# Hybrid encoder layer on one core: the output projection as seven half-size products, with its weight sums kept in DRAM

## The chip, the cores and the metric

The kernel runs on one core of a Trainium2 chip. The metric is the device time of one execution in microseconds (us), as the median of several runs. TensorE (PE in the profile) multiplies; VectorE (DVE), ScalarE (ACT) and GpSimd (POOL) do the element-wise work; SyncE (SP) issues most of the transfers.

## The reference

One layer of an encoder over 1024 tokens of 1024 features, all in float32:

```
u   = x @ W_in
mix = concat(retention(u), windowed_attention(u))     # 8 + 8 heads of 64
h   = LN1(alpha * x + mix @ W_out)
f   = SwiGLU(h) + sigmoid(h @ W_pg) * (p @ W_pe)
out = LN2(alpha * h + f)
```

The change concerns `mix @ W_out`, the product of two 1024x1024 matrices, and LN1 behind it. What follows directly, `h @ W_pg` (the gate) and `p @ W_pe` (the embedding, whose 256 inputs a token are few), plays a part in the order of work.

## The kernel before, in words

A float32 product is made of three passes of a split operand: each operand is a rounded high part and the low rest (`split`, L74: a ScalarE copy writes the high part, L75, a VectorE subtraction the low part, L76), and `mm3` (L81 to L83) multiplies high by high, high by low and low by high into one bank of PSUM. A matmul takes 128 rows of the inner index and makes 128 tokens by 512 features. There are eight banks, two each of the tags mm, s, t and o.

The mixers (retention and attention, four pairs) run first. TensorE's order there is laid down by hand: large matmuls are queued and `take` pulls some of them between the small ones; `side` holds small jobs that are given out at a count of such ticks. One kind of side job prepares weights: `put` splits a sum of weight slices on ScalarE and VectorE and SyncE writes both parts to DRAM. The gate's weights are prepared so (`presplit_gate`), because the gate is calculated by seven products of half-size matrices in place of eight, on sums of quarters of h and of W_pg.

The output projection has 8 inner slices (KT), 8 token tiles and 2 halves of the features. The mixers' output is split on the spot and so are the 8 slices of W_out, after they are loaded. The first four token tiles go together, slice by slice, into all eight banks; then tiles 4 to 7 one after another into two banks. `zpart` (L753) adds a tile to alpha times x, `ln_stats` takes its statistics, and `ln1_apply` does LN1: a power on GpSimd (L763) and two VectorE passes (L768, L769). `to_hT` transposes a tile on TensorE (L784, into banks) and splits it (L785, L786) into the four quarters HB of h. LN1 and transposes of tiles 0 to 3 lie in the middle of the products of tiles 4 to 7; tiles 4 and 5 are transposed behind the projection, tiles 6 and 7 inside gate product 1.

Then the gate. `product` (L891 to L893) multiplies four token tiles by four slices of one operand, into four banks; gate product 1 and product 2 share a set of banks (mm, s), product 5 has the other (t, o). Between the tiles of product 2 stand the embedding tiles (`first_tile`, `embed`): six matmuls into a bank of t or o, a sigmoid on ScalarE, a multiplication by the bank on VectorE (L948), an addition (L950). `t_sums` makes the operand sums of the gate's further products on VectorE (L860 to L867), each split in turn; product 5 needs the first of them, TT[1], which takes in all eight tiles of h. The SwiGLU part follows and takes more than half of the kernel's time.

Up to gate product 1 only TensorE's order in the mixers is by hand; from there on TensorE's and SyncE's order is as written. The other engines' orders are made by a scheduler: each engine works strictly in its own order.

## Time and profile before

| | |
|---|---|
| median of 3 runs | 1204.29 us (1204.23 to 1205.2) |
| the profiled execution | 1208.0 us, span 1206.2 us |
| granted TensorE clock, mean | 0.998 |
| TensorE busy | 1192.5 us |
| output projection on TensorE | 375.36 to 466.61 us |
| first matmul of gate product 1, of product 5 | 468.27, 497.39 us |
| hardware-issued DMA, GpSimd-issued DMA | 160.61 MB, 16.78 MB |

The profile is of one execution; its times count from the span's start. Rows of the timeline have the start, the length, the engine, the line, the operation, output and inputs by their names (buffer numbers left out), the shape, and in brackets the idle time ahead and what ended it. A matmul's length includes the drain of its pipeline, so that matmuls overlap; the distance between starts is what one takes.

### The profile page before, as it was taken

Reading aid. Unit: us, or ns where it says so; the run is one execution under the profiler, and the core shown is the slowest. Engines: PE = TensorE matmul, PEld = TensorE weight load, DVE = VectorE, ACT = ScalarE, POOL = GpSimd, SP = SyncE. Lnnn points to the kernel's source line nnn. Section 1 sums busy time; section 2 is a strip of 40 time slices with the busy share of each in tenths; the row PEclk is TensorE's granted clock in tenths of the full one; section 3 lists DMA queues with packets and bytes.
Section 4 is the critical chain, followed back from the end, with each engine's and each line's share of the span. In section 5 each row is a group of like instructions: output and inputs, shape, how many; then the busy total and the mean of one; then the engine's idle time right before and its main releaser. Section 6 shows DMA issues by size and latency. Waiting matters only on the chain.

```text
span 1206.2 us, 16452 instructions
## 1 busy us (share of the span) xinstructions
PE 1192.5 (99%) x5940; PEld 994.1 (82%) x5940; DVE 735.6 (61%) x1262; ACT 507.6 (42%) x958; POOL 363.1 (30%) x342
## 2 busy tenths in 40 slices
PE   9999999999999999999999999999999999999997
PEld 6888888888888888888888888888888888888885
DVE  4633788866645387946855554455554565775677
ACT  4665237665775124303423323233323324562463
POOL 2001020202010021001765565646656432034232
PEclk9999999999999999999999999999999999999999
DMA  6233635410103216656233222332133159999976
GB/s 249 83 110 141 249 135 195 151 40 20 35 18 122 91 50 229 255 202 220 89 132 131 79 79 105 131 132 79 63 121 131 70 178 300 375 274 218 258 178 199
DMA packets 70034, 178.45 MB, mean 148 GB/s; under 512 B 8128, under 2 KB 12352, under 8 KB 69952
## 3 DMA queue, kind: packets, MB, share of 16 engines
q1 hardware_dynamic: 61312, 160.61, 37.3%
q0 software_dynamic: 8640, 16.78, 8.0%
q8 instruction: 47, 0.77, 0.3%
q14 instruction: 35, 0.29, 0.1%
HBM read 124.67 MB, written 47.45 MB: 143 GB/s over the span
## 4 chain that ended last, share of the span: by engine, by line
PE 95%; DVE 2%; DMA 1%; issue 1%; ACT 1%; DVEq 0%; SPq 0%; ACTq 0%
PE bmm L81 7%; PE bmm L83 7%; PE bmm L82 7%; PE bs L893 5%; PE bs L891 5%; PE bs L892 5%; PE bmm L891 5%; PE bmm L892 5%; PE bmm L893 5%; PE bt L891 5%; PE bt L893 5%; PE bt L892 5%; PE bo L891 4%; PE bo L893 4%; PE bo L892 4%; PE bo L557 2%
## 5 line engine op out<-in xcount | busy, mean ns | idle before, releaser
L81 PE MATMUL bmm<-H,w 128*128 128x512 f32 x240 | 97.0, 404 | 1.4 <-ACT H L75 1.4
L83 PE MATMUL bmm<-H,w 128*128 128x512 f32 x240 | 94.4, 393 | 0.0
L82 PE MATMUL bmm<-H,w 128*128 128x512 f32 x240 | 94.0, 392 | 0.0
L1050 POOL TENSOR_TENSOR H<-ln 128x512 f32<-128x512 f32 x22 | 28.9, 1313 | 180.9 <-ACT w L75 98.0
L76 DVE TENSOR_TENSOR w<-raw,w 128x512 fp32r<-128x512 f32 x64 | 51.0, 804 | 51.3 <-ACT w L75 50.8
L1080 POOL TENSOR_TENSOR ev<-ev 128x512 f32<-128x512 f32 x33 | 55.0, 1666 | 90.5 <-DVE ev L1095 39.4
L76 DVE TENSOR_TENSOR w<-H,w 128x512 fp32r<-128x512 f32 x44 | 41.0, 932 | 62.5 <-ACT w L75 62.5
L518 POOL COPY sc<-skb 128x1 f32<-128x1 f32 x64 | 14.3, 229 | 193.0 <-PE bt L545 143.9
L1078 ACT ACTIVATE ev<-ev 128x512 f32<-128x512 f32 x33 | 20.9, 632 | 102.7 <-DVE ev L1095 102.7
L1084 POOL TENSOR_TENSOR ev<-ev,ev 128x512 f32<-128x512 f32 x44 | 62.7, 1437 | 2.6
L76 DVE TENSOR_TENSOR u<-H,u 128x512 fp32r<-128x512 f32 x47 | 36.7, 781 | 37.7 <-ACT u L75 37.4
L81 PEld LDWEIGHTS bmm<-H,w 128*128 128x128 f32 x240 | 45.2, 188 | 11.6 <-ACT H L75 2.4
L83 PEld LDWEIGHTS bmm<-H,w 128*128 128x128 f32 x240 | 45.2, 188 | 10.0
L523 DVE CUSTOM_DVE_ANT_0 sc<-cst,bs,skb 128x384 f32<-128x384 f32 (+1 forms) x64 | 34.8, 577 | 28.8 <-PE bs L522 27.0
L75 ACT ACTIVATE w<-raw 128x512 fp32r<-128x512 f32 x64 | 39.3, 624 | 30.2 <-PE bo L83 12.4
L82 PEld LDWEIGHTS bmm<-H,w 128*128 128x128 f32 x240 | 45.3, 189 | 7.8
L527 ACT ACTIVATE sc<-sc,st 128x385 f32<-128x385 f32 (+1 forms) x64 | 37.2, 584 | 32.2 <-DVE st L525 32.2
L75 ACT ACTIVATE u<-H 128x512 fp32r<-128x512 f32 x47 | 29.6, 630 | 44.6 <-PE bs L893 8.1
L763 POOL TENSOR_TENSOR stt<-stt,cst 128x1 f32<-128x1 f32 x8 | 11.6, 1456 | 101.0 <-DVE stt L762 101.0
L479 POOL TENSOR_TENSOR sm<-sm,cst 128x8 f32<-128x8 f32 x8 | 14.3, 1783 | 88.3 <-DVE sm L478 88.3
L1054 POOL TENSOR_TENSOR H<-raw,H 128x512 f32<-128x512 f32 x22 | 37.3, 1697 | 0.0
L1051 POOL TENSOR_TENSOR H<-H,raw 128x512 f32<-128x512 f32 x22 | 35.7, 1624 | 1.7
(807 smaller groups left out, 3748.1 us busy)
## 6 DMA issues: line engine op xcount, KB each, us to landing
ad<-ev SPq DMA_DIRECT2D x33, 512.0 KB, 2.6
pgd<-pro SPq DMA_DIRECT2D x28, 512.0 KB, 2.9
raw<-in_w_gu SPq DMA_DIRECT2D x22, 512.0 KB, 4.3
ln<-in_w_gu SPq DMA_DIRECT2D x22, 512.0 KB, 3.6
raw<-ad SPq DMA_DIRECT2D x40, 256.0 KB, 5.8
ln<-ad SPq DMA_DIRECT2D x37, 256.0 KB, 6.2
H<-in_w_dn SPq DMA_DIRECT2D x33, 256.0 KB, 6.1
raw<-in_w_mt SPq DMA_DIRECT2D x14, 512.0 KB, 3.8
```

Of the source, the lines that this page charges most:

```text
L75: act.activation(hi, raw, AF.Copy)
L76: dve.tensor_tensor(lo, raw, hi.bitcast(F32), ALU.subtract)
L81: pe.matmul(o, lh, rh, start=start, stop=False)
L82: pe.matmul(o, lh, rl, start=False, stop=False)
L83: recent[0] = pe.matmul(o, ll, rh, start=False, stop=stop).ins.name
L527: act.activation(sc[g][:, :nk + 1], sc[g][:, :nk + 1], AF.Exp, bias=st_[:, 1, j, g:g + 1], accum_out=st_[:, 2, j, g:g + 1])
L891: pe.matmul(o, lh, rh, start=start, stop=False, skip_group_check=True)
L892: pe.matmul(o, lh, rl, start=False, stop=False, skip_group_check=True)
L893: pe.matmul(o, ll, rh, start=False, stop=stop, skip_group_check=True)
L1054: pool.tensor_tensor(s[3], a(0, 1), s[0], ALU.subtract)
L1080: pool.tensor_tensor(c[:, 1, :], c[:, 0, :], c[:, 1, :], ALU.mult)
L1084: pool.tensor_tensor(self.ev[dst][:, 0, :], left, right, op)
```

## The change

The output projection becomes seven products too. Token half i and inner half j of the mixers' output are quarters A(i,j); their sums (a11, a12, s1 to s4, a22) are made and split at the end of the mixers. The seven operands of W_out are made during the mixers by new side jobs: of each pair of inner slices seven sums or slices are split by `put` and written to DRAM (`wod`), and `out_w` streams four slices a product back, as the gate's are. Products run in the order 1, 2, 6, 5, 3, 7, 4, each 48 matmuls, on two sets of four banks. Products 1 to 3, 5 and 6 are combined from copies of the banks; for tiles 4 to 7, twelve of the additions are done by transfers that GpSimd issues and that add to their target. x is loaded straight into the accumulators.

LN1's statistics are sums: the last addition of a tile's half also sums its row (`complete`, L854), ScalarE sums the other half in a copy (`halfsum`, L857), and squares with a sum (L863) in place of `bn_stats`. Line numbers shift: L892 and L893 are now the split of a transposed tile, L867 and L868 the two passes of LN1, L973 to L980 the operand sums, L1021 and L1023 the multiplication and addition of an embedding tile, L71 and L72 the split, L761 to L763 and L77 to L79 the matmuls.

The tiles' transposes move: tile 0 behind product 7, tile 1 inside product 4, tile 2 behind it; tile 3 inside gate product 1, tile 4 behind it, tiles 5 and 6 inside gate product 2, tile 7 behind the first embedding tile. The other three embedding tiles come after it, where three of four stood between the tiles of product 2. The banks' tags mm and t change places from the end of the mixers on, so that embedding tiles use mm and o, and product 5 too. The core of the diff:

```diff
+    def presplit_out(kt, ops, start, gap, raws=()):
...
+        def step(p, k, k2, i):
+            x = hold[k]
+            if k2 is not None:
+                behind(dve.tensor_tensor(x, x, hold[k2], ALU.add))
+            put(x, ops[i % len(ops)], wod[p - 1, kt])
+        todo = ((1, 0, None), (2, 2, None), (3, 3, None), (5, 0, 1), (7, 1, 3), (6, 0, 3), (4, 0, 2))
...
         side.extend(presplit_small())
+        for kt in range(2):
+            side.extend(presplit_out(kt, [twin(spare[1]), small_op], 17.5 + 31 * kt, 3.4))
...
+            if i == 2:
+                late = [ytile(6), ytile(7)]
+                side.extend(presplit_out(2, [twin(late[1].bitcast(F32R))], 2, 3.4, late[:1]))
+            elif i == 3:
+                side.extend(presplit_out(3, [twin(bt([P, S], "aq", 3, F32R))], 2, 3.4, [bt([P, S], "rkq", 3)]))
...
+    ROLE.update(mm="t", t="mm")
...
+    def complete(t, h, b):
+        dve.tensor_tensor_reduce(half(t, h), half(t, h), b, 1.0, 0.0, ALU.add, ALU.add, stts[t][:, h:h + 1])
+    def halfsum(t, h):
+        act.activation(ct([P, HF], "sg", 2), half(t, h), AF.Copy, accum_out=stts[t][:, h:h + 1])
...
-    for t in range(4, NT):
-        new_acc()
-        bb = [bank(k) for k in ("mm", "s")]
-        for kt in range(KT):
-            for h in range(2):
-                outp(bb[h], t, h, kt)
-            if kt == 3:
-                ln1_apply(t - 4)
-                to_hT(t - 4)
...
+    product(5, X, True, s1o)
+    for k in range(4):
+        dve.tensor_tensor(half(4 + k, 1), half(4 + k, 1), X[k], ALU.add)
+        pool.dma_start(half(4 + k, 0), s1[k], accum_op=ALU.add)
+        pool.dma_start(half(4 + k, 1), ns1[k], accum_op=ALU.add)
...
+    product(7, Z, False, s3o)
+    for k in range(4):
+        act.activation(nb[k], Z[k], AF.Copy, scale=-1.0)
+        pool.dma_start(half(4 + k, 1), nb[k], accum_op=ALU.add)
+        halfsum(4 + k, 1)
+    to_hT(0, ("mm", "s"))
+    product(4, Z, False, a22, [lambda: None, lambda: None, lambda: to_hT(1, ("mm", "s"))])
+    for k in range(4):
+        complete(4 + k, 0, Z[k])
+        ln1_apply(4 + k)
+    to_hT(2, ("mm", "s"))
...
-    product(1, X, True, HB[0, 0], [lambda t=t: to_hT(t) for t in (6, 7)], True)
+    product(1, X, True, HB[0, 0], [lambda: None, lambda: to_hT(3)])
...
+    to_hT(4)
...
+        if k in (0, 2):
+            to_hT(5 + k // 2)
+    first_tile(0)
+    to_hT(7)
+    steps = t_sums()
+    for k in range(4):
         steps[k]()
         if k:
-            first_tile(k - 1)
+            first_tile(k)
     gate_w(5, (2, 3))
-    first_tile(3)
```

TensorE, from the last tile's transposes to gate product 5, before (numbers behind the names tell tiles apart):

```order
L784 MATMUL bt_4368<-cst,acc_4164 128x128 x4
L784 MATMUL bo_4375<-cst,acc_4164 128x128 x4
...
L81 MATMUL bt_4456<-w_4321,p_4325 128x512
...
L81 MATMUL bo_4485<-w_4321,p_4327 128x512
...
L81 MATMUL bt_4514<-w_4321,p_4467 128x512
...
L81 MATMUL bo_4529<-w_4321,p_4496 128x512
...
L891 MATMUL bt_4548<-w_4407,H_4417 128x512
```

and now:

```order
L77 MATMUL bmm_4643<-w_4467,p_4471 128x512
...
L891 MATMUL bmm_4656<-cst,acc_3961 128x128 x4
L891 MATMUL bo_4663<-cst,acc_3961 128x128 x4
L77 MATMUL bo_4686<-w_4467,p_4473 128x512
...
L77 MATMUL bmm_4703<-w_4467,p_4654 128x512
...
L77 MATMUL bo_4718<-w_4467,p_4697 128x512
...
L761 MATMUL bmm_4741<-w_4540,H_4671 128x512
...
L761 MATMUL bo_4743<-w_4540,H_4671 128x512
```

Before, the rest of gate product 1, all of product 2 and the four embedding tiles stand between the transposes and product 5; now three embedding tiles do (six matmuls each, the rows left out), and the first group of product 5 in each bank comes right behind.

VectorE, from the split of the last transposed tile to the multiplication of the last embedding tile, before:

```order
L786 TENSOR_TENSOR h_4264<-bt_4368,h_4264 128x4x128
L786 TENSOR_TENSOR h_4265<-bo_4375,h_4265 128x4x128
L860 TENSOR_TENSOR ln_4432<-h_4264,h0a_3922 128x1024
L860 TENSOR_TENSOR ln_4450<-h_4264,h0a_3922 128x1024
...
L76 TENSOR_TENSOR H_4417<-ln_4432,H_4417 128x1024
...
L948 TENSOR_TENSOR sg_4463<-sg_4463,bt_4456 128x512
...
L948 TENSOR_TENSOR sg_4536<-sg_4536,bo_4529 128x512
```

and now:

```order
L893 TENSOR_TENSOR h_4538<-bmm_4656,h_4538 128x4x128
L893 TENSOR_TENSOR h_4539<-bo_4663,h_4539 128x4x128
L973 TENSOR_TENSOR ln_4674<-h_4538,h0a_4233 128x1024
...
L1021 TENSOR_TENSOR sg_4693<-sg_4693,bo_4686 128x512
L72 TENSOR_TENSOR H_4671<-ln_4674,H_4671 128x1024
L72 TENSOR_TENSOR H_4671<-ln_4680,H_4671 128x1024
...
L1021 TENSOR_TENSOR sg_4710<-sg_4710,bmm_4703 128x512
...
L980 TENSOR_TENSOR ln_4680<-ln_4680,h_4539 128x1024
L1021 TENSOR_TENSOR sg_4725<-sg_4725,bo_4718 128x512
```

VectorE's rows are nearly the same in kind and order; between the last L893 and the last L1021 stand, counted with the rows left out, 13 of 128x1024 and 4 of 128x512.

ScalarE, around the last additions to tiles 4 to 7 (acc_3952, acc_3955, acc_3958 and acc_3961), where before only L785 and L787 stood:

```order
L785 ACTIVATE h_4264<-bt_4269 128x4x128
L785 ACTIVATE h_4265<-bo_4276 128x4x128
L787 ACTIVATE acc_3924<-acc_3924 128x1024
L785 ACTIVATE h_4264<-bt_4284 128x4x128
L785 ACTIVATE h_4265<-bo_4291 128x4x128
```

and now:

```order
L944 ACTIVATE H_4024<-bmm_3964 128x512
L944 ACTIVATE H_4024<-bmm_3965 128x512
L863 ACTIVATE sg_4224,stt_3820<-acc_4046,stt_3820 128x512
L863 ACTIVATE sg_4226,stt_3820<-acc_4046,stt_3820 128x512
L857 ACTIVATE sg_4293,stt_3821<-acc_3952 128x512
L857 ACTIVATE sg_4297,stt_3822<-acc_3955 128x512
L944 ACTIVATE H_4024<-bo_3966 128x512
L944 ACTIVATE H_4024<-bo_3967 128x512
L892 ACTIVATE h0a_4233<-bt_4307 128x4x128
...
L857 ACTIVATE sg_4301,stt_3823<-acc_3958 128x512
```

The row sums L857 of tiles 4 and 5, which read what the transfers have added, stand ahead of the copies L944 of product 7's banks 2 and 3.

263 lines of the change are left out of this document (146 added, 117 removed).

## The prediction

> **What bounds the kernel now.** I read the page's busy table first, then the waits of TensorE, then the busy time by stage, then TensorE's and VectorE's rows around the end of the output projection. Columns of the page: busy us, share of the span, instructions.
>
> ```profile
> span 1206.2 us, 16452 instructions
> PE 1192.5 (99%) x5940; PEld 994.1 (82%) x5940; DVE 735.6 (61%) x1262; ACT 507.6 (42%) x958; POOL 363.1 (30%) x342
> ```
>
> TensorE is busy for 1192.5 of 1206.2 us. What it waits for (us in total, times, longest) is little:
>
> ```profile
> PE bmm L81 <- ACT H L75: 1.4, 1, 1.4
> PE bs L521 <- DVE pt L436: 1.3, 1, 1.3
> PE bo L146 <- POOL sq L143: 1.3, 1, 1.3
> PE bmm L82 <- DVE w L76: 0.2, 1, 0.2
> ```
>
> So a matmul less is a gain one for one, and a new wait of TensorE a loss one for one; nothing else on the chip has to change for that. By stage (us, then busy us and instructions of TensorE, its weight loads, VectorE, ScalarE, GpSimd, then clock, DMA share, GB/s):
>
> ```profile
> 67.00:130.00 63.00, 63.00 (x388) 52.52 (x388) 23.40 (x63) 33.61 (x79) 5.08 (x20) 1.00 0.43 154
> 240.00:305.00 65.00, 65.00 (x460) 56.58 (x459) 40.22 (x112) 36.23 (x88) 9.21 (x22) 1.00 0.12 41
> 305.00:368.00 63.00, 62.91 (x429) 54.31 (x429) 33.41 (x98) 45.76 (x92) 5.45 (x14) 1.00 0.09 31
> 430.00:478.00 48.00, 48.00 (x242) 40.33 (x241) 36.16 (x55) 15.79 (x24) 8.74 (x6) 1.00 0.41 145
> 478.00:500.00 22.00, 22.00 (x99) 18.22 (x98) 21.93 (x24) 10.00 (x13) 0.00 (x0) 1.00 0.53 179
> ```
>
> The mixers (the first three rows) leave VectorE and ScalarE a third or more of the time. In the last row VectorE is busy 21.93 of 22 us: it is full there, and TensorE still never waits. That stretch makes the operand sums of the gate's products, and it is where this change cuts the cover.
>
> **What the change removes.** The output projection runs from the row at 375.36 to the first transpose of tile 4:
>
> ```profile
> 375.36 0.39 PE L81 MATMUL bmm<-w,H 128*128 128x512 f32 x1
> 375.58 0.39 PE L82 MATMUL bmm<-w,H 128*128 128x512 f32 x1
> 375.81 0.39 PE L83 MATMUL bmm<-w,H 128*128 128x512 f32 x1
> ...
> 466.61 0.60 PE L784 MATMUL bt<-cst,acc 128*128 128x128 f32 x4
> ```
>
> Matmuls start every 0.227 us (the 0.39 is the length of one, with its drain). Before there are 8 slices x 8 tiles x 2 halves x 3 passes = 384; afterwards 7 products x 4 x 4 x 3 = 336. 48 x 0.227 = **10.9 us** less.
>
> **What it adds in the mixers.** 28 weight slices get a ScalarE copy, a VectorE subtraction and a 512 KB write, and 16 of them an addition. At the 0.71 us of ScalarE and 0.68 of VectorE that 128x512 rows further down show, the first stage takes on 14 slices, some 10 us of ScalarE and 15 of VectorE (33.61 and 23.40 of 63 become about 44 and 38); each of the later two stages takes 7, some 5 and 8 us. TensorE's order there is the same, row for row. With that much room I take 0; if an engine stands at the wrong moment, up to 2 us. The splits of w_out that vanish stood beside a full TensorE: 0 saved, but for the 0.2 us wait shown. Products 1 to 7 each have 10.9 us to bring in 2 MB and to empty four banks (four 128x512 operations, 2.7 us): 0, up to 0.5.
>
> **Stop B: gate product 5.** In the kernel before, the transposes of the last tile and the first matmul of gate product 5 stand so on TensorE:
>
> ```profile
> 474.74 0.60 PE L784 MATMUL bt<-cst,acc 128*128 128x128 f32 x4
> 475.18 0.60 PE L784 MATMUL bo<-cst,acc 128*128 128x128 f32 x4
> ...
> 497.16 0.39 PE L83 MATMUL bo<-u,p 128*128 128x512 f32 x1
> 497.39 0.39 PE L891 MATMUL bt<-w,H 128*128 128x512 f32 x1
> ```
>
> and on VectorE, which between them splits the last tile (L786), adds up the operand (L860 to L862) and splits it (L76):
>
> ```profile
> 476.01 0.69 DVE L786 TENSOR_TENSOR h<-bt,h 128x512 fp32r<-128x512 f32 x1 [1.21 <-ACT h L785]
> 476.62 0.68 DVE L786 TENSOR_TENSOR h<-bo,h 128x512 fp32r<-128x512 f32 x1
> 477.21 2.35 DVE L860 TENSOR_TENSOR ln<-h,h0a 128x1024 f32<-128x1024 f32 x2
> 479.48 2.36 DVE L861 TENSOR_TENSOR ln<-ln,h 128x1024 f32<-128x1024 f32 x2
> 481.75 2.35 DVE L862 TENSOR_TENSOR ln<-ln,h0a 128x1024 f32<-128x1024 f32 x2
> 484.10 1.23 DVE L76 TENSOR_TENSOR H<-ln,H 128x1024 fp32r<-128x1024 f32 x1
> 487.77 1.22 DVE L76 TENSOR_TENSOR H<-ln,H 128x1024 fp32r<-128x1024 f32 x1
> 488.90 0.68 DVE L948 TENSOR_TENSOR sg<-sg,bt 128x512 f32<-128x512 f32 x1
> ```
>
> TensorE has 497.39 - 474.74 = 22.65 us of work between the two; the first half of the operand is ready at 484.10 + 1.23 = 485.3, 10.6 us after the transposes begin, the second at 489.0, 14.3 us after. Nothing waits. The change moves that last transpose behind gate product 2 and the first embedding tile. What is left on TensorE is 8 transposes (0.87) and three embedding tiles of six matmuls (3 x 6 x 0.227): 4.95 us. The same sums then hold product 5 up by at least 10.6 - 4.95 = 5.6 us.
>
> It doesn't end there. Gate product 5 begins with one matmul group into each of four banks, and the third and fourth of the embedding tiles sit in two of those (as the rows above show for before: the tiles write bt and bo, and so does product 5). Each is freed by its multiplication with the gate, L1021, and the last of these stands on VectorE, by the order shown above, behind 2 splits, 13 operations of 128x1024 and 4 of 128x512, and is one more itself. Those rows start 1.135 and 0.60 us after one another: 13 x 1.135 + 7 x 0.60 = 19.0. They begin 1.3 us after the transposes (474.74 to 476.01): 20.3 us. TensorE reaches that bank after 4.95 us and three groups of three matmuls (2.04): **20.3 - 7.0 = 13.3 us** lost. Two loads of the embeddings' inputs, which now wait for buffers later, cost some tenths that this swallows. Bounds: 5.6 (only the operand's first half binds) and 14.5 (one more 128x1024 operation, ScalarE's part of the split, adds to it).
>
> **Stop A: gate product 1.** The projection's last additions are done by accumulating transfers that GpSimd issues. The nearest rows, from the end of the kernel, with those of the row sums on ScalarE, GpSimd's power and the two passes of LN1 (median or mean ns of one, first and last start):
>
> ```profile
> L1376 POOL DMA_DIRECT2D acc<-R x12: 867/872/1458, 1071.6 to 1117.2; - x12
> DMA to landing us min/median/max: 4.4/5.6/8.9
> L1295 ACT ACTIVATE sg<-acc,stt x14: 706/709/726, 1164.8 to 1195.0; 128x512 f32<-128x512 f32 x14
> L1295 ACT ACTIVATION_READ_ACCUMULATOR sg<-acc,stt x14: 185/187/188, 1165.5 to 1195.6; 128x1 f32 x14
> L763 POOL TENSOR_TENSOR stt<-stt,cst x8: 1285/1522/1523, 425.0 to 470.1; 128x1 f32<-128x1 f32 x8
> L768 DVE SCALAR_TENSOR_TENSOR acc<-acc,stt,ln 128x1024 f32<-128x1024 f32 x6 | 7.6, 1276 | 0.0
> L769 DVE SCALAR_TENSOR_TENSOR acc<-acc,stt,ln 128x1024 f32<-128x1024 f32 x6 | 7.6, 1278 | 0.9 <-POOL stt L763 0.9
> ```
>
> Product 7 ends at 375.4 + 6 x 10.9 = 440.7. ScalarE then has to copy its banks 2 and 3 for the last two transfers, but ahead of these copies stands the row sum of tile 5 (L857), which waits for the transfer of bank 1. Bank 1 is full at half of product 7, 435.3, and copied at about 436.3; landed at 440.7 to 441.9 if GpSimd issues it at once. It stands behind the power of tile 2 there, so I take 443. The sum and two copies take it to 445, the two issues (0.87 each) to 446.5, and landing to about 450.5. Then come a row sum (0.8), two squares for tile 4 (1.6), two statistics, L867 (1.28), the power (1.52), L868 (1.28), tile 6's addition (0.76) and the split L893 (0.68), with the statistics 8.4: 458.9. TensorE is through product 4 and three tiles' transposes at 454.4 and needs the bank that this L893 frees: **4.5 us**; 2.0 with the shorter landing and a free GpSimd, 7 with landings of 8.9 us. Its second group needs the bank of the next L893, which VectorE reaches after two L867, one L868, two additions, a split and six statistics, 6.6 us later; TensorE fills 2.7 of these: **3.9 us**, less where the first stop is short. Together 8.4, and I take 8.0; bounds 2 and 11.
>
> **The sum.** -10.9 + 8.0 + 13.3 = **+10.4 us**. The profiled execution took 1208.0 (span 1206.2), 3.7 over the median of 1204.29; I add the sum to the median: **1214.7 us**. Stages behind product 5 keep their order and find their inputs early, so they shift as a block.
>
> **The clock.** TensorE's start shows what a long pause does:
>
> ```profile
> 7.80 0.63 PE L81 MATMUL bo<-H,w 128*128 128x512 f32 x1
> 8.22 0.63 PE L82 MATMUL bmm<-H,w 128*128 128x512 f32 x1
> ...
> 10.24 0.39 PE L83 MATMUL bt<-H,w 128*128 128x512 f32 x1
> 10.47 0.39 PE L82 MATMUL bo<-H,w 128*128 128x512 f32 x1
> ...
> 176.42 0.39 PE L521 MATMUL bs<-k,aq 128*128 128x256 f32 x1 [1.33 <-DVE pt L436]
> ```
>
> Matmuls start 0.42 us apart until about 10, 0.23 afterwards; behind a pause of 1.33 us they are quick at once. No row shows a pause of 3 to 5 us. If each stop (A, and B with its few groups between waits) were followed by 3.7 us at the slow rate, as the start was, each would cost 3.7 x (1 - 0.23/0.42) = 1.7 us more, 3.4 in all: 1218.1. [...]
>
> **The rivals.** (1) As summed: 1214.7, its own range 1209 to 1219: 0.50. (2) The clock falls back at the stops: 1218.1: 0.20. For it: the first 10 us. Against: stop A is cut by work. (3) The transfers land before their sums are called for, stop A is nil: -10.9 + 13.3 = +2.4, 1206.7. For it: DMA is 0.41 busy there. Against: ScalarE and GpSimd serve them in order. 0.09, half of it counted as no change. (4) Faster: gate product 5 waits for its operand alone. The place is VectorE behind the last transpose, the price 5.6 instead of 13.3: the embedding tiles' multiplications would have to be through before the second half of the sums, so that no bank binds. With A at its lower bounds (2 or less) that is -10.9 + 5.6 + 2 = -3.3, 1201.0; with no A 1199.0; it decides where both stops together fall under 10.9. Against: VectorE works in its order, and 1.135 us is measured. With all waits hidden it is 1193.4. 0.13. (5) The mixers pay for the slices, 2 to 5 us on top: 1217 to 1220: 0.08. For it: ScalarE is at 45.76 of 63 in the third stage. Against: TensorE is full beside it, 62.91 of 63.
>
> A measurement of this kernel can tell about 0.2%, 2.4 us. Slower: 0.50 + 0.20 + 0.08 less the low edge of (1), 0.77 in all; same: 0.10, from (3) and that edge; faster: 0.13. The range reaches from case (3)'s low side to the clock's case with a dear stop A: 1203 to 1220.
>
> **What would show it.** In the changed profile: a projection of 65 us of TensorE work and no waits before 454; a wait of gate product 1 for L893 of 3 to 6 us, then one of 3 to 4; a wait of gate product 5 for ScalarE's split, then for L1021, 12 to 14 in all; matmul starts 0.42 us apart behind them if (2) holds. I am wrong if TensorE has no wait at L1021's banks, if L857 never holds ScalarE, or if waits appear before 375.

## The result

The changed kernel takes **1234.2 us** (median of 4 runs, 1231.06 to 1235.2) against 1204.49 for the kernel before beside it (1204.23 to 1205.2): 1.0241 times as long, 95% interval 1.0221 to 1.0261. The prediction had the direction, slower, and missed the size: it forecast 10.4 us more and a top of 1220, and 29.7 came. The profiled execution took 1233.38 us with a span of 1231.3, against 1208.0 and 1206.2 before: 25.1 us by spans, for which the text below accounts. The other 4.6 lie in the executions that were profiled: the one of before is 3.5 over its median, the one of after 0.8 under its own, and 0.3 is the difference between a time and its span.

### The profile page after: what moved, and what is told of

The parts are those of the page before. It is cut to its first block, busy times and chain, and to the rows that moved or that the text cites. A ratio compares the mean times of both kernels' runs of the same rounds, so it can differ in the third digit from the quotient of the medians.

```text
span 1231.3 us, 16701 instructions
## 1 busy us (share of the span) xinstructions
PE 1193.4 (97%) x5892; PEld 990.0 (80%) x5892; DVE 760.2 (62%) x1334; ACT 551.1 (45%) x1058; POOL 371.5 (30%) x354
## 4 chain that ended last, share of the span: by engine, by line
PE 79%; DMA 8%; DVE 6%; issue 3%; ACT 2%; POOL 2%; DVEq 0%; POOLq 0%; ACTq 0%; SPq 0%
PE bmm L77 5%; PE bmm L79 5%; PE bmm L78 5%; PE bs L761 5%; PE bs L762 5%; PE bs L763 5%; PE bt L761 5%; PE bt L762 4%; PE bt L763 4%; PE bmm L761 4%; PE bmm L762 4%; PE bmm L763 4%; PE bo L762 4%; PE bo L761 4%; PE bo L763 4%
## 5 line engine op out<-in xcount | busy, mean ns | idle before, releaser
L77 PE MATMUL bmm<-H,w 128*128 128x512 f32 x240 | 97.8, 408 | 3.5 <-ACT w L71 3.5
L79 PE MATMUL bmm<-H,w 128*128 128x512 f32 x240 | 94.6, 394 | 0.0
L72 DVE TENSOR_TENSOR w<-H,w 128x512 fp32r<-128x512 f32 x44 | 39.8, 905 | 63.4 <-ACT w L71 63.2
L72 DVE TENSOR_TENSOR w<-raw,w 128x512 fp32r<-128x512 f32 x56 | 43.9, 790 | 46.6 <-ACT w L71 46.4
L72 DVE TENSOR_TENSOR u<-H,u 128x512 fp32r<-128x512 f32 x47 | 36.2, 771 | 41.8 <-ACT u L71 41.5
L77 PEld LDWEIGHTS bmm<-H,w 128*128 128x128 f32 x240 | 45.6, 190 | 13.8 <-ACT w L71 3.9
L79 PEld LDWEIGHTS bmm<-H,w 128*128 128x128 f32 x240 | 45.4, 189 | 10.3 <-DVE w L72 0.2
L71 ACT ACTIVATE u<-H 128x512 fp32r<-128x512 f32 x47 | 29.6, 631 | 44.5 <-PE bt L763 9.0
L71 ACT ACTIVATE w<-raw 128x512 fp32r<-128x512 f32 x56 | 34.5, 624 | 13.9 <-PE bo L79 8.3
L71 ACT ACTIVATE w<-H 128x512 fp32r<-128x512 f32 x44 | 27.4, 622 | 22.0 <-PE bt L763 6.3
```

The costliest lines, as they stand in the source:

```text
L71: act.activation(hi, raw, AF.Copy)
L72: dve.tensor_tensor(lo, raw, hi.bitcast(F32), ALU.subtract)
L77: pe.matmul(o, lh, rh, start=start, stop=False)
L79: recent[0] = pe.matmul(o, ll, rh, start=False, stop=stop).ins.name
```

## The profile after

The page of the changed kernel, busy time and instructions of the engines:

```profile
span 1231.3 us, 16701 instructions
PE 1193.4 (97%) x5892; PEld 990.0 (80%) x5892; DVE 760.2 (62%) x1334; ACT 551.1 (45%) x1058; POOL 371.5 (30%) x354
```

48 matmuls are gone as predicted (5940 to 5892), and yet TensorE is busy 0.9 us longer than before and idle for 37.9 us instead of 13.7. So two things are to be found: 24 us of waiting, and matmuls that take longer. What TensorE waits for, the longest groups (us in total, times, longest):

```profile
PE bt L761 <- DVE h0a L893: 6.4, 2, 5.3
PE bmm L77 <- ACT w L71: 3.5, 1, 3.5
PE bmm L761 <- DVE sg L1021: 3.0, 1, 3.0
PE bo L761 <- DVE sg L1021: 2.8, 1, 2.8
PE bmm L761 <- ACT H L71: 2.4, 1, 2.4
PE bmm L761 <- DMA u<-wod: 1.5, 1, 1.5
PE bmm L761 <- DMA w<-wod: 1.4, 1, 1.4
```

The first row is stop A, the rows of L1021 and of ACT H are stop B, both foreseen. ACT w L71 is a stop in the mixers and the two DMA rows are a stop in the projection; those were not. By stage (columns as in the prediction):

```profile
67.00:130.00 63.00, 63.00 (x387) 52.54 (x386) 33.55 (x79) 37.10 (x86) 5.78 (x20) 1.00 0.64 234
130.00:175.00 45.00, 41.49 (x245) 35.37 (x244) 35.68 (x68) 17.82 (x34) 7.43 (x6) 0.96 0.68 257
420.00:430.00 10.00, 10.00 (x46) 8.26 (x44) 4.26 (x7) 2.17 (x6) 3.07 (x4) 1.00 1.09 297
430.00:440.00 10.00, 7.11 (x24) 4.96 (x23) 4.97 (x17) 5.29 (x14) 1.52 (x3) 0.85 1.06 359
430.00:478.00 48.00, 37.73 (x156) 29.24 (x155) 31.18 (x62) 23.96 (x56) 9.88 (x12) 0.89 0.72 232
500.00:520.00 20.00, 9.75 (x36) 6.16 (x34) 19.84 (x22) 6.36 (x9) 0.00 (x0) 0.80 0.62 223
```

The mixers' first stage (67 to 130) is as full as before; the wait comes behind it, at 140. From 420 to 440 the DMA engines are full (1.09, 1.06); before, the share was 0.18 from 400 to 440, and 0.41 only behind it, from 430 to 478. And where TensorE waits, its granted clock falls: 0.85, 0.89, 0.80. The rows of TensorE show that too; the start of the projection's first product, product 7, its end, stop A, the start and end of stop B, and gate product 6:

```profile
378.55 0.39 PE L761 MATMUL bt<-w,H 128*128 128x512 f32 x1
...
434.50 0.50 PE L761 MATMUL bmm<-w,h 128*128 128x512 f32 x1 [1.39 <-DMA w<-wod]
436.96 0.79 PE L761 MATMUL bmm<-u,h 128*128 128x512 f32 x1 [1.50 <-DMA u<-wod]
...
448.87 0.60 PE L891 MATMUL bt<-cst,acc 128*128 128x128 f32 x4
...
469.21 0.80 PE L761 MATMUL bt<-w,h0a 128*128 128x512 f32 x1 [5.29 <-DVE h0a L893]
...
473.64 0.63 PE L762 MATMUL bt<-u,h0a 128*128 128x512 f32 x1
474.07 0.59 PE L763 MATMUL bt<-u,h0a 128*128 128x512 f32 x1
...
509.55 0.50 PE L761 MATMUL bmm<-w,H 128*128 128x512 f32 x1 [2.38 <-ACT H L71]
509.89 0.40 PE L762 MATMUL bmm<-w,H 128*128 128x512 f32 x1
...
520.54 0.80 PE L761 MATMUL bo<-w,H 128*128 128x512 f32 x1 [2.81 <-DVE sg L1021]
521.13 0.63 PE L762 MATMUL bo<-w,H 128*128 128x512 f32 x1
...
531.93 0.39 PE L761 MATMUL bt<-w,H 128*128 128x512 f32 x1
```

Behind the pauses of 5.29 and 2.81 us, and behind 1.39 and 1.50 close together, matmuls start 0.43 us apart (473.64 to 474.07), not 0.23; the two behind 2.38 alone are quick (509.55 and 509.89, 0.50 and 0.40 long). In all 41 matmuls start at the slow distance behind five stops (140, 437, 469, 515 and 521 us), which is 41 x 0.20 = 8 us of TensorE's time. That is the clock case of the prediction; how much of the 8 us delays anything is another question, answered further down.

The account, before to after, each row from one start to another. Product 1 begins at 378.55, the projection before began at 375.36: **+3.2** in the mixers. (The mixers lose more than that. In this execution TensorE came out of the start 2.4 us ahead of before: its thirteenth f32 matmul of 128x512 begins at 8.51, before at 10.93. So 5.6 are lost behind the start.) Six products of 48 x 0.227 = 10.88 would end at 443.8; product 7 ends at 448.87: **+5.0**. In product 4 TensorE waits 1.0 for a bank: **+1.4** with the restart (the second matmul starts 0.34 us behind the first, at 456.71, the third 0.23 behind the second). Stop A, with a short second wait and its slow matmuls, from 462.88 to 499.92 us for 27.5 of work: **+9.5**. From 499.92, the transposes of the last tile, to gate product 6 at 531.93 are 32.0 us for 15.8 of work: **+16.2**. With the 10.9 removed that is +24.4; the SwiGLU's first matmul moves from 568.14 to 592.31, +24.2. Behind it come another 0.9, of which 0.57 is one wait, at 1205.81.

Stop A and the wait in product 4 have one cause, and ScalarE's rows show it:

```profile
455.11 0.63 ACT L857 ACTIVATE sg<-acc 128x512 f32<-128x512 f32 x1 [5.88 <-DMA acc<-H]
455.74 1.06 ACT L944 ACTIVATE H<-bo 128x512 f32<-128x512 f32 x2
```

The row sum L857 waits 5.88 us for an accumulating transfer, and the copies L944 of product 7's banks 2 and 3 stand behind it. Product 4 waits for those banks, and the last two transfers, which tiles 6 and 7 need, start from these copies.

## The experiments

All times are medians beside runs of the kernel before on the same chip; "the change" is the changed kernel at 1234.2. The medians of the kernel before beside them lie between 1204.9 and 1205.7, beside the change at 1204.49, so a difference from the change can be off by up to 1 us. From lowest to highest the executions of these kernels lie 2 to 10 us apart, those of the kernel before 2 to 7. So a single place is read from the profile's rows and the whole from the medians. The intervals of e2, e4 and e5 touch that of the change: what these three show, they show by rows.

### Each place alone

**e1: the first stage's weight sums.** Only slices of the first inner pair are made; the products read these in the place of the second pair's, so a quarter of each product has the wrong weights.

```diff
-        for kt in range(2):
+        for kt in range(1):
...
-            stream(wod[p - 1, kt])
+            stream(wod[p - 1, 0 if kt == 1 else kt])
```

> The side jobs of one of the four pairs of inner slices (the second) are left out; its loads read the first pair's sums, so part of the product is calculated from the wrong weights. Theory (ScalarE's copy of the first projected tile stands behind the put that last reads that tile's memory, and the puts follow each other only as fast as their writes land): the stop of 3.5 us at 140 us and the 1.4 us of slow matmuls behind it are gone, 4 to 6 us less. Rival (VectorE and ScalarE have simply too much to do in that stage, the two slices' share of it small): less than 2 us.

Measured: 1227.43 (1226.84 to 1230.98), ratio 1.019, interval 1.0174 to 1.0206: 6.8 less than the change, a little above what was expected. No wait is left at 140 us and product 1 begins at 372.36. So the mixers pay for the second set of seven slices in the first stage. How, the rows of ScalarE's split of a weight (L570) in the change show, idle time ahead of it by what ended it (us, times):

```profile
DMA wod<-pro: 6.0, 3
DMA ped<-pro: 5.7, 3
```

ScalarE has time enough (37.10 of 63), but it works in its order, and the split into the operand tile `pro` waits there until the last write out of that tile has landed. The embedding's small operands (`ped`) and the sums (`wod`) use the same tile. Behind the split stands the one that TensorE waits for. e1 takes the work and the writes of seven slices away together; that the writes are what counts is read from these rows.

**e6: a tile of their own for the sums.**

```diff
+        more_op = a_tile([P, 2, HF], "pro", "A1", F32R)
-            side.extend(presplit_out(kt, [twin(spare[1]), small_op], 17.5 + 31 * kt, 3.4))
+            side.extend(presplit_out(kt, [twin(spare[1]), more_op], 17.5 + 31 * kt, 3.4))
```

> The sums of the first two pairs of slices get a second operand tile of their own; the gate's small weights keep the one that both shared. Theory (each put waits for the write of the put before it, 3 to 6 us, and ScalarE's order carries that to the projected tile): the stop at 140 us falls from 3.5 to below 1.5 us, with its slow matmuls 3 to 6 us less. Rival (the memory the last put reads, not the operand's write, or the loads of raw weights, is late): the stop stays within 1 us.

Measured: 1249.69 (1248.36 to 1252.2), ratio 1.0369, interval 1.0353 to 1.0385. A miss, and the wrong way: one stop of 16.65 us at 156.65, again for ScalarE's L71. By the program, the new tile comes out of the ring that the gate's side jobs use; in ScalarE's rows of e6 the split waits 5.4 and 4.4 us for writes out of `pro` (124.84 and 130.38 us). That the shared ring makes this stop was not tried apart from it. **e9: the small operands sooner** (tick 10 for 18).

```diff
-(ticks[0] + 18 + 15 * n + at, f)
+(ticks[0] + 10 + 15 * n + at, f)
```

> The side jobs that prepare the embedding's small operands start 8 ticks earlier (at tick 10 instead of 18); nothing else moves. Theory (the stop at 140 us is ScalarE's copy of the first projected tile, which waits for the last of these puts because it uses the memory that this put reads): the last put ends 5 to 8 us sooner, the stop of 3.5 us and its slow matmuls are gone or below 1 us, 3 to 6 us less. Rival (the puts of the weight sums and the writes behind them set the pace, and the earlier ones only queue): the stop stays above 2.5 us.

Measured: 1234.26 (1230.91 to 1240.88), ratio 1.0237, interval 1.0207 to 1.0267: nothing gained. The stop at 140 is gone, and this row has come in its place:

```profile
PE bo L460 <- DVE kv L419: 3.5, 1, 3.5
```

VectorE waits there 2.9 us for ScalarE's part of a split, which waits 3.3 us for the same kind of write (`pgd` out of `pro`). The rival holds: by the rows it is the chain of write, split, write in engines that work in order, and not the place of one job.

**e2: the loads of x ahead of product 5's weights.**

```diff
-    out_w(5)
     for k in range(4):
         load_x(4 + k)
+    out_w(5)
```

> The loads of x for tiles 4 to 7 (2 MB) are issued ahead of product 5's weights instead of behind them, some 8 us earlier. Theory (between 400 and 440 us more is asked of the transfers than they bring, and product 7's weights come late for that): product 7's two waits (2.9 us) and its slow matmuls fall by half or more, 2 to 5 us less in all. Rival (product 7's weights wait for their buffers and for SyncE's order, not for the traffic): no change, within 1 us.

Measured: 1230.32 (1229.39 to 1231.46), ratio 1.0209, interval 1.0193 to 1.0224, 3.9 less than the change. Product 7 still waits 1.51 and 0.45 for its weights, 2.0 of the 2.9 us and so less of a fall than was expected; product 5, whose weights now come behind x, waits 0.36.

**e13: product 5's eight accumulating transfers become additions on VectorE;** the four negated copies go.

```diff
-    for k in range(4):
-        act.activation(ns1[k], s1[k], AF.Copy, scale=-1.0)
...
-        pool.dma_start(half(4 + k, 0), s1[k], accum_op=ALU.add)
-        pool.dma_start(half(4 + k, 1), ns1[k], accum_op=ALU.add)
+        dve.tensor_tensor(half(4 + k, 0), half(4 + k, 0), s1[k], ALU.add)
+        dve.tensor_tensor(half(4 + k, 1), half(4 + k, 1), s1[k], ALU.subtract)
```

> Product 5's eight accumulating transfers become eight additions on VectorE (about 0.60 us each, as the additions of the same width beside them), and the four negated copies on ScalarE go; nothing else of the change is undone. Theory (product 7's weights came late because four loads of input tiles, 4 MB, and these eight transfers, 2 MB written by accumulation, lie in the same 40 us as the weights): without the eight the weight loads land earlier, the two waits before product 7 (2.9 us in the change, with half-rate matmuls behind them) fall to under 1.5 and the kernel takes 1229 to 1232 us. Rival (the eight are nothing beside the loads of the tiles and of the weights): the waits stay at 2.5 to 3.0 and the time stays within 1 us of 1233.

Measured: 1226.54 (1221.35 to 1228.59), ratio 1.0169, interval 1.0146 to 1.0192: 7.7 less than the change, more than expected. The two windows of the change that were over-full are in e13:

```profile
420.00:430.00 10.00, 10.00 (x46) 8.29 (x45) 8.96 (x18) 4.05 (x11) 0.00 (x0) 1.00 1.02 389
430.00:440.00 10.00, 10.00 (x46) 8.28 (x45) 7.38 (x16) 4.34 (x12) 2.44 (x4) 1.00 0.81 274
```

TensorE is full through both, and the DMA engines move 389 GB/s where they moved 297 with the transfers, at the same share. A load of x lands after 6.9 us (median) instead of 8.9 (14.5 at the longest, 7.4 here). Product 7 has no wait for weights left, and gate product 1 begins 7.8 us earlier (461.46 for 469.21), after a wait of 2.9 instead of 5.3: stop A was itself late through these transfers. The theory holds: without the eight, product 7 waits no more, though the loads of x stand where they stood; moving the loads alone (e2) leaves 2.0 us of waiting.

**e3: stop A without transfers.** Product 7's results are added by VectorE in the bank's place:

```diff
-        act.activation(nb[k], Z[k], AF.Copy, scale=-1.0)
-        pool.dma_start(half(4 + k, 1), nb[k], accum_op=ALU.add)
+        dve.scalar_tensor_tensor(half(4 + k, 1), Z[k], -1.0, half(4 + k, 1), ALU.mult, ALU.add)
```

> Product 7 is added to tiles 4 to 7 on VectorE out of the bank, without the ScalarE copy and without the four accumulating transfers. Theory (stop A is the chain copy, transfer, row sum in ScalarE's order): gate product 1's waits fall from 6.4 us to below 3, with the slow matmuls behind them 5 to 8 us less. Rival (VectorE's own queue for LN1 of tiles 4 to 7 decides, and gets 2.4 us longer): 0 to 2 us less, or slower.

Measured: 1227.19 (1224.9 to 1230.17), ratio 1.0184, interval 1.0164 to 1.0204, 7.0 less than the change. The two waits of gate product 1 (6.4 in all) are one of 2.4, with no slow matmul behind it. ScalarE's copies and the landing were the larger part of stop A, as predicted.

**e4: stop B with the embedding tiles between the operand's sums.** The sums' first half, three embedding tiles, then the rest:

```diff
-    for k in range(4):
+    for k in range(2):
+        steps[k]()
+    for k in range(1, 4):
+        first_tile(k)
+    for k in range(2, 4):
         steps[k]()
-        if k:
-            first_tile(k)
```

> Only the order in which VectorE works changes: the multiplications and additions of the last three embedding tiles stand ahead of the second operand's sums (TT[2]) instead of among them. Theory (stop B is the banks that those multiplications free, behind 13 wide operations): the waits of gate product 5 for L1021 (5.8 us) and the slow matmuls behind them go, the wait for its operand (3.4 us) stays: 6 to 9 us less. Rival (VectorE's whole amount of work behind the last transpose decides; what product 5 gains, product 6 waits for): less than 2 us.

Measured: 1229.63 (1227.17 to 1234.47), ratio 1.0207, interval 1.0178 to 1.0237. From the last tile's transposes to gate product 6 it takes 26.5 instead of 32.0, and the two waits at the embedding's banks (5.8) are 1.8: the multiplications that stood behind the sums in VectorE's order did hold the banks. The median falls by 4.6, less than expected; the slow matmuls stayed, behind a pause of 1.83 that follows one of 1.97.

**e5: the clock.** TensorE is kept busy through stop B by 30 matmuls into a bank that nobody reads:

```diff
+    def idle(n):
+        for _ in range(n):
+            pe.matmul(fb, HB[0, 0][:, 0, 0, :P], HB[1, 0][:, 0, 0, :], start=True, stop=True, skip_group_check=True)
+    idle(8)
...
+            if kt == 0 and k in (1, 3):
+                idle(11)
```

> 30 matmuls whose result nothing reads are put on TensorE where it waits in stop B: 8 ahead of gate product 5, 11 ahead of its second and 11 ahead of its fourth bank; each lot is shorter than the wait it stands in. Theory (the clock: TensorE starts matmuls 0.43 us apart after its pauses, whatever it then does): the first dozen matmuls behind the last wait of stop B start 0.23 us apart, and product 6 begins 2 to 3 us sooner behind the last transposes; 1.5 to 4 us less in all. Rival (what comes late behind the pauses is operands, banks or weights, the clock is a reading only): the matmuls behind it are as far apart as before, or wait; no gain, or up to 1 us more.

Measured: 1229.57 (1226.86 to 1234.13), ratio 1.0203, interval 1.0178 to 1.0229. Behind the second bank, TensorE's rows in e5 (L1077 is the added matmuls' line):

```profile
521.92 2.66 PE L1077 MATMUL bt<-h0b,h0a 128*128 128x512 f32 x11
526.16 0.50 PE L761 MATMUL bo<-w,H 128*128 128x512 f32 x1 [1.59 <-DVE sg L1021]
526.50 0.40 PE L762 MATMUL bo<-w,H 128*128 128x512 f32 x1
526.74 0.39 PE L763 MATMUL bo<-w,H 128*128 128x512 f32 x1
```

The bank comes no sooner, and the matmuls behind it start 0.23 us apart where they started 0.43 apart in the change. Transposes to gate product 6: 29.6 for 32.0. So 2.4 us of stop B are the clock alone, since nothing else was changed; that slow matmuls follow a stop because TensorE paused is shown here by rows.

**e7: the last transposes early.** Tiles 4 to 7 are transposed one place sooner each, and the sums come before the embedding tiles.

```diff
-    product(1, X, True, HB[0, 0], [lambda: None, lambda: to_hT(3)])
+    product(1, X, True, HB[0, 0], [lambda: None, lambda: to_hT(3), lambda: to_hT(4)])
...
-    to_hT(4)
+    to_hT(5)
...
-        if k in (0, 2):
-            to_hT(5 + k // 2)
+        if k < 2:
+            to_hT(6 + k)
+        if k == 1:
+            steps = t_sums()
+            steps[0]()
+            steps[1]()
```

> The transposes of tiles 4 to 7 go forward on TensorE: tile 4 into gate product 1, tile 5 behind it, tiles 6 and 7 behind the first and second group of product 2, and the sums for product 5 stand ahead of the embedding tiles. Theory (stop B exists because only 5 us of matmuls stand between the last transpose and product 5, where VectorE needs 10.6 us to the first half and the banks wait behind that): 10.8 us more cover, no wait of product 5 above 1 us, no slow matmuls there, 10 to 16 us less. Rival (tile 7's LN1 is only just ready where its transpose stood; moved forward, TensorE waits for it there): the waits reappear at the transposes, less than 5 us gained.

Measured: 1224.25 (1221.6 to 1229.22), ratio 1.0169, interval 1.0141 to 1.0197: 10.0 less than the change, the low end of what was expected. Gate product 5 waits no longer for sums; 1.9 for an embedding input is what is left. e7 also holds e4's order, with the last three embedding tiles ahead of the second operand's sums, so the 10.0 of stop B's 16.2 belong to both: e4's order alone gave 4.6, and if the two add up, 5.4 are the earlier transposes.

### Put together

**e8: e6, e2, e13, e3 and e7 in one.**

```diff
+        more_op = a_tile([P, 2, HF], "pro", "A1", F32R)
...
-    out_w(5)
...
+        dve.tensor_tensor(half(4 + k, 0), half(4 + k, 0), s1[k], ALU.add)
...
+        dve.scalar_tensor_tensor(half(4 + k, 1), Z[k], -1.0, half(4 + k, 1), ALU.mult, ALU.add)
...
+            to_hT(6 + k)
```

> Together: the second operand tile, x of tiles 4 to 7 earlier, all twelve accumulating transfers replaced by VectorE additions, and the early transposes. Theory (mixers, weights of product 7, stop A, stop B are separate losses): 23 to 33 us less than the change, 1201 to 1211 us, about the kernel before; below it if the sums of the losses hold in full. Rival (VectorE's amount of work between 400 and 520 us binds, the waits move from one place to the next): more than 1215 us.

Measured: 1224.14 (1222.93 to 1225.14), ratio 1.0154, interval 1.0139 to 1.0169. The forecast missed because e6's tile is in it, with a stop of 16.5; behind the mixers stop A is 2.4 and of stop B only a wait of 1.84 for an embedding input and one of 0.44 are left. **e10** leaves the mixers as in the change, and also puts an embedding tile behind each tile of gate product 2 and tile 2's transpose ahead of LN1 of tiles 4 to 7:

```diff
-            first_tile(k)
+            first_tile(k - 1)
...
-    product(4, Z, False, a22, [lambda: None, lambda: None, lambda: to_hT(1, ("mm", "s"))])
+    product(4, Z, False, a22, [lambda: None, lambda: None, lambda: to_hT(1, ("mm", "s")), lambda: to_hT(2, ("mm", "s"))])
```

> x of tiles 4 to 7 earlier, all twelve accumulating transfers replaced by VectorE additions, the early transposes with the embedding tiles among product 2 as in the kernel before, and tile 2's transposes placed ahead of LN1 of tiles 4 to 7 in the program. The mixers as in the change. Theory (weights of product 7, stop A and stop B are separate and all curable): only the stop at 140 us is left, 1234 - 5 - 8 - 15 = 1202 to 1209 us. Rival (VectorE's amount of work binds): above 1212 us.

Measured: 1206.9 (10 runs, 1203.04 to 1212.49), ratio 1.0014, interval 0.9996 to 1.0032. 27 of the change's 30 us are back, with every wait of the projection and stop A gone. **e11** is e10 with e9's edit:

```diff
-(ticks[0] + 18 + 15 * n + at, f)
+(ticks[0] + 10 + 15 * n + at, f)
```

> The kernel of the run before with the small operands' side jobs 8 ticks earlier. Theory: no stop is left that the kernel before doesn't have, 10.9 us of matmuls less: 1195 to 1201 us, faster than before. Rival (the stop in the mixers is not in these jobs' place but in the weight sums): 1202 us or more, no better than the run before by over 2 us.

Measured: 1207.46 (12 runs), ratio 1.0017, interval 1.0003 to 1.0031: as in e9, a wait of 3.6 at L460 takes the place of the one removed. **e12** is e10 with the second set of sums moved into the mixers' third stage, behind those of the third:

```diff
-        for kt in range(2):
+        for kt in range(1):
...
-                side.extend(presplit_out(2, [twin(late[1].bitcast(F32R))], 2, 3.4, late[:1]))
+                side.extend(presplit_out(2, [twin(late[1].bitcast(F32R))], 2, 3.0, late[:1]))
+                side.extend(presplit_out(1, [twin(late[1].bitcast(F32R))], 24, 3.0, late[:1]))
```

> The kernel e10 (no accumulating transfers, earlier x and transposes), with the weight sums of the second pair of slices moved out of the first stage: they follow those of the third pair, from 240 us on, in the same operand tile. Theory (two pairs of slices and the small operands are too much for the operand tiles of the first stage, whose puts wait for each other's writes; from 240 us on the transfers are idle two thirds of the time and writes land soon): no stop at 140 us, and a stop of at most 1 us later: 1198 to 1203 us, faster than before. Rival (14 puts in one operand tile hold up ScalarE from 240 us on): the stop comes back there with 2 us or more, 1204 us or above.

Measured: 1205.64 (12 runs, 1202.34 to 1210.69) beside 1205.68, ratio 1.0002, interval 0.9987 to 1.0017. The stop at 140 is gone, and new short ones stand where the moved sums are now: 0.7, 1.3 and 0.4 us at 303, 314 and 327. A product less, and no gain: what is left had to be found.

### The last stop

e12's longest wait is 2.62 us at the first matmul of gate product 7, with seven slow starts behind it. VectorE is full from 480 to 510 us there (busy 30.00 of 30 us).

**e14: four of VectorE's additions go to GpSimd** (the embedding's, L1020). The expectation puts them at 1.1 us each; the rows say 0.60.

```diff
-        dve.tensor_tensor(accs[t][:, sl], accs[t][:, sl], sg, ALU.add)
+        adder.tensor_tensor(accs[t][:, sl], accs[t][:, sl], sg, ALU.add)
...
-        embed(k, 0, X[k], wpe, "to"[k % 2], pt[k])
+        embed(k, 0, X[k], wpe, "to"[k % 2], pt[k], pool)
```

> As e12, and the first four additions of the embedding onto the residual go from VectorE to GpSimd, whose pool is idle there; they are read by stores alone soon. Theory (what is left of the second stop in e12, 2.6 us before gate product 7's operand and about 2.9 us of half-rate matmuls behind it, is VectorE's total work from 477 to 518 us, of which four additions of 1.1 us are 4.5 us): the stop before that operand is gone or under 1 us, the matmuls behind it stand 0.23 us apart, and the kernel takes 1198 to 1203 us, faster than before by 0.2 to 0.6%. Rival (what is left comes from the order in which the operands are split and summed, or GpSimd's additions on the same tiles slow VectorE's down): the stop stays at 2 us or more and the time stays at 1204 to 1207.

Measured: 1206.5 (12 runs, 1202.94 to 1211.31), ratio 1.0004, interval 0.999 to 1.0018. VectorE's timeline in e12, where no other engine adds:

```profile
485.13 1.22 DVE L72 TENSOR_TENSOR H<-ln,H 128x1024 fp32r<-128x1024 f32 x1
486.26 1.22 DVE L972 TENSOR_TENSOR ln<-ln,h0a 128x1024 f32<-128x1024 f32 x1
```

The same engine in e14 (two instructions to a row):

```profile
487.36 3.42 DVE L72 TENSOR_TENSOR H<-ln,H 128x1024 fp32r<-128x1024 f32 x2
491.90 4.20 DVE L976 TENSOR_TENSOR ln<-h,ln 128x1024 f32<-128x1024 f32 x2
```

And GpSimd in e14:

```profile
487.58 2.12 POOL L1020 TENSOR_TENSOR acc<-acc,sg 128x512 f32<-128x512 f32 x1 [6.37 <-DVE sg L1018]
491.51 3.50 POOL L1020 TENSOR_TENSOR acc<-acc,sg 128x512 f32<-128x512 f32 x2 [1.81 <-issue]
```

One of VectorE's additions of 128x1024 takes 1.13 us in e12 (485.13 to 486.26), two with the drain 2.35; beside GpSimd's additions two take 3.42 and 4.20. With a third place (3.45) that is 4.0 us for 2.4 saved, and the stop went from gate product 7 to gate product 5 (2.31). The rival holds in so far: VectorE's additions and splits of 128x1024 take longer where GpSimd's additions run beside them (behind the last of these, two take 2.35 again, at 496.02). Why they do, the rows do not show.

**e15 and e16: the additions as accumulating transfers**, all four, or two with the other two late on VectorE.

```diff
-        dve.tensor_tensor(accs[t][:, sl], accs[t][:, sl], sg, ALU.add)
+        if by_dma:
+            pool.dma_start(accs[t][:, sl], sg, accum_op=ALU.add)
+        else:
+            dve.tensor_tensor(accs[t][:, sl], accs[t][:, sl], sg, ALU.add)
```

> As e12, and the embedding's first four additions onto the residual are done by accumulating transfers from GpSimd's queue in place of VectorE or GpSimd, so that no other engine computes beside VectorE. In e14 the four left VectorE (4 times 0.60 us) but VectorE's own instructions beside GpSimd's took 1.07, 1.07 and 1.85 us longer, so nothing was won. Theory (the last stop is VectorE's work between 478 and 515 us, and e14 lost its 2.4 us to contention with GpSimd): the two waits before product 5 (1.1 and 0.7 in e12) and the 2.6 us before gate product 7's operand fall by 1.5 to 2.4 us together with the half-rate matmuls behind them, VectorE's rows of 1024 columns stand 1.13 us apart all through, and the kernel takes 1200 to 1203 us, faster than before by 0.2 to 0.4%. Rival (the order of the operands, or the transfers collide with the loads of the weights, which already take a share of 0.95 from 490 to 500 us): waits of 2 us or more stay, on a weight or a tile, and the time stays at 1204 to 1207.

> As e15, but only the first two of the four additions are transfers; the other two stay on VectorE and are issued after gate product 6, behind all of its work for the operands. The same theory expects the same waits as in e15 and 1200 to 1203 us, since the two are out of the stretch from 478 to 515 us as well; the rival that transfers collide with the weights expects this one to be 0.5 to 2 us faster than e15, and the rival of the operands' order 1204 to 1207.

Measured: 1207.5 (12 runs), ratio 1.002, interval 1.001 to 1.003, and 1211.94 (6 runs), ratio 1.0053, interval 1.0037 to 1.0069. Both missed: the fourth sigmoid writes a tile that the second transfer still reads (5.7 us to landing), VectorE waits for that sigmoid in its order, and TensorE stops for 5.8 and 5.5 us. **e17** keeps two additions in place and two late, without transfers:

```diff
-        dve.tensor_tensor(accs[t][:, sl], accs[t][:, sl], sg, ALU.add)
+        add = lambda: dve.tensor_tensor(accs[t][:, sl], accs[t][:, sl], sg, ALU.add)
+        add() if late is None or t < 2 else late.append(add)
...
     product(6, Y, True, TT[2], steps[6:8])
+    for f in late_adds:
+        f()
```

> As e12, but the last two of the embedding's four additions are issued on VectorE after gate product 6 in place of before the operands of gate product 5; no transfer and no GpSimd addition is added, and the first two additions stay, so that the tile of the fourth sigmoid comes free as in e12 (in e15 and e16 it waited for a transfer of 5.7 us, which made a new stop of 5.5 to 5.8 us). VectorE has 2 times 0.60 = 1.2 us less to do before gate product 7's operand. Theory (VectorE's total work ends last there): the wait at that operand falls from 2.6 to about 1.4 us or less; pauses of 1.4 us alone were followed by matmuls at the full rate in the change, so the half-rate matmuls behind it go too (2.9 us), and the kernel takes 1200 to 1203 us, 0.2 to 0.4% faster than before. Rival (something else than VectorE's work sets that operand): the wait stays at 2.3 us or more and the time at 1204 to 1207.

Measured: 1207.16 (7 runs), ratio 1.0029, interval 1.0015 to 1.0042: a miss, the wait grew to 4.5. But VectorE's timeline of e17 says what it is for:

```profile
511.40 1.28 DVE L1020 TENSOR_TENSOR acc<-acc,sg 128x512 f32<-128x512 f32 x2
512.60 1.22 DVE L72 TENSOR_TENSOR h<-ln,h 128x1024 fp32r<-128x1024 f32 x1
513.74 1.28 DVE L1032 TENSOR_TENSOR H<-raw,bt 128x512 f32<-128x512 f32 x2
```

TensorE's in the same run:

```profile
514.52 0.76 PE L762 MATMUL bt<-w,H 128*128 128x512 f32 x1 [4.55 <-issue]
```

TensorE had nothing left to do at 509.97 and goes on at 514.52, as the first read of bank bt (L1032, from 513.74, one is 0.6 to 0.7) ends. Gate product 7 accumulates in the banks that these reads take gate product 6's sum from. It waits for the reads, and the reads wait in VectorE's order behind operand sums that nobody needs before gate product 4 and, here, behind the two additions.

**e18: the reads first** (e12 otherwise).

```diff
-    product(6, Y, True, TT[2], steps[6:8])
+    product(6, Y, True, TT[2])
...
     add4(u2, s1, Y)
+    steps[6]()
+    steps[7]()
     product(7, Y, False, TT[3])
```

> As e12, with one edit: the additions that read gate product 6's four banks (line 1031) are issued ahead of the last two steps of the operands' sums, which only gate product 4 needs, some 10 us later. Theory after e17 (there VectorE had 1.2 us less to do before these additions in its program, the two late additions were put ahead of them by the scheduler all the same, the first of the four reads began at 513.74 us and TensorE went on at 514.52): the last stop is gate product 7, which accumulates in the banks that these additions read first, waiting for them behind VectorE's operand work in VectorE's order. Then the wait of 2.6 us (e12) falls under 0.5, the matmuls behind it stand 0.23 us apart, and the kernel takes 1199 to 1202 us, 0.3 to 0.5% faster than before. Rival (VectorE's total work before that point is what ends last, in whatever order): the wait moves to gate product 7's operand (1.5 us or more at L72's tiles) and the time stays at 1204 to 1207.

Measured: **1200.68 us** (10 runs, 1199.08 to 1202.69) beside 1204.92, ratio 0.9963, interval 0.9952 to 0.9974. The page of e18:

```profile
span 1197.3 us, 16673 instructions
PE 1181.1 (99%) x5892; PEld 984.5 (82%) x5892; DVE 769.3 (64%) x1346; ACT 545.8 (46%) x1050; POOL 359.7 (30%) x342
```

Its longest waits of TensorE:

```profile
PE bs L517 <- DVE pt L432: 2.0, 2, 1.3
PE bo L142 <- POOL sq L139: 1.3, 1, 1.3
PE bt L404 <- ACT ptr L543: 1.3, 1, 1.3
```

And the first of the reads on VectorE, which e12 makes at 513.12:

```profile
503.90 0.67 DVE L1031 TENSOR_TENSOR H<-raw,bt 128x512 f32<-128x512 f32 x1
```

The wait at gate product 7 is gone and no pause is longer than 1.3 us. VectorE's work is the same in e12 and e18 (770.2 and 769.3 us), so its total was not the bound there; its order was. The seven products are worth having, by 0.4%, when little waits for them: TensorE is busy 1192.5 - 1181.1 = 11.4 us less than before. By spans e18 gains 8.9 us, by medians 4.2. The difference lies again in which executions were profiled (1199.08, the lowest of e18; 1208.0 of before, 3.5 over the median that stands beside the change); the medians decide. Of the 8.9, 3.4 lie at the start, where the thirteenth f32 matmul of 128x512 begins at 10.93 before and at 7.51 in e18. What makes the executions scatter was not tried; the profiled ones differ in this start and in a wait near the end, for an addition on VectorE, which is absent in e18 and 3.95 us in e14.

## Why the prediction was wrong, point by point

**Removed: 10.9.** Right: 48 matmuls are gone, and TensorE's busy time falls by 11.4 in e18, where it no longer waits.

**Stop B, 13.3.** Right in mechanism and size. The last bank came free 20.6 us after the transposes (499.92 to 520.54), where 20.3 was forecast; with 7.0 of work in between that is 13.6 lost. The other 2.6 of the 16.2 are the restart (0.59 us from the first start to the second) and eleven slow starts behind it. The banks at L1021 and the order on VectorE were the cause (e4), as was the place of the last transpose (e7, beside e4).

**Stop A, 8.0.** Right in mechanism, near in size: 9.5. L857 held ScalarE, to 455.1 where 443 was taken; product 7 itself ended 8.2 late. The second group's bank came 6.5 us behind the first (469.21 to 475.74), where 6.6 was forecast; slow matmuls filled most of that, so the second wait is 1.1 and not 3.9. e3 shows the chain of copy, transfer and landing. e13 adds what the prediction did not have: that chain was also late because the DMA engines were full.

**"Products 1 to 7 each have 10.9 us to bring in 2 MB and to empty four banks (four 128x512 operations, 2.7 us): 0, up to 0.5."** This step failed: 5.0 at product 7 and 1.4 in product 4, where at most 0.5 was allowed for. 2 MB in 10.9 us is 190 GB/s, and the step gave no other ground for its 0. It left out that 16 loads of x (4 MB) and the eight accumulating transfers share the same 40 us, 400 to 440, where the DMA share is then 1.05 and a load of x lands after 8.9 us, at times 14.5. e13 and e2 show both parts. The 0.41 that rival (3) goes by is of another stretch and of the kernel before: the change adds these streams to it. Product 4's wait is for a bank that L944 had not emptied, four short copies as the step has it, but behind L857.

**"With that much room I take 0; if an engine stands at the wrong moment, up to 2 us."** This failed too: +3.2 by the rows, and 6.8 by e1's medians, or 378.55 - 372.36 = 6.2 by where product 1 begins, of which 1.0 lies at the start (the thirteenth f32 matmul of 128x512 begins at 7.53 in e1, at 8.51 in the change). The engines were even less busy from 67 to 130 than forecast, ScalarE 37.10 for about 44 and VectorE 33.55 for about 38, in part because two of the 14 slices came later. ("A third or more" was also too much for ScalarE: 45.76 of 63 leaves 27%.) But the mean over a stage doesn't show a chain: a write of 512 KB, then a split into the tile that it read, in an engine where TensorE's own split stands behind. By its own sign, waits before 375, the prediction was wrong here. That product 1 begins only 3.2 late is owed to the start of the two profiled executions. ScalarE's first split waits there for the first load of the input, before:

```profile
5.67 1.29 ACT L75 ACTIVATE H<-rv 128x512 fp32r<-128x512 f32 x2 [3.66 <-DMA rv<-in_xT]
```

and in the change:

```profile
3.96 0.63 ACT L71 ACTIVATE H<-rv 128x512 fp32r<-128x512 f32 x1 [1.95 <-DMA rv<-in_xT]
```

The load came sooner, and fewer slow matmuls followed (starts 0.43 us apart up to 9.93 before, up to 6.52 in the change): the 2.4 us of the account. It may be part of the 3.5 by which the profiled execution of before lies over its median; that no run shows.

**The clock, 0.20 at 3.4 us.** The case came true: five stops, not two, each with 5 to 11 slow starts, 1.0 to 2.2 us for the 1.7 forecast. The argument against it, that stop A is cut by work, doesn't hold: eleven slow starts follow its first wait. But not all of the 8 us delay something. Behind stop A's first wait and behind 515 us the next wait ends when VectorE frees a bank, by rows that need nothing of these matmuls (it is busy from 464.4 to 475.7 and from 500.1 to 520.5 but for 0.4 us), so that the 16 slow starts there only shorten that wait. What is left is 2.6 at the end of stop B (2.4 in e5) and up to 1.4 each at 140 and 437: some 5 us. At A and B together, where the prediction had 3.4, it is 2.6.

**The sum.** -10.9 + 9.5 + 13.6 for what was foreseen is +12.2, beside the +10.4 of the forecast. What came on top is product 7 and product 4, with 1.4 of slow matmuls in them (6.4), the mixers (3.2), and the slow matmuls at the end of stop B (2.6): 12.2. Together 24.4.

**The rivals.** (3) and (4), without a stop A or with B at its operand alone, are out. (5), mixers that pay 2 to 5, and (2) came true both, on top of (1); the range let each come alone, and none let a stop come in the projection's loads.

## What to carry to other kernels

Where TensorE is 99% busy, a product less is a gain only when every engine that serves it has its work in the right order: look for each read of a bank, each write out of a shared tile and each transfer in a queue, and ask what stands ahead of it, for a stage's mean busy time doesn't tell. Add a new stream to all that already flows in the same microseconds, accumulating transfers included. And count a pause of TensorE of 2.6 us or more (39 of 43 had slow matmuls behind them here) at its length plus these matmuls, 1.0 to 2.2 us a stop in the change, unless another wait stands right behind and takes them up.
